# A hybrid SSM/attention layer on one core: squares summed before the token sums, loads and stores on other queues, weight copies in a later stage

## The chip, the cores and the metric

The kernel runs on one core of a Trainium2 chip as a single launch. The metric is the time of one execution on the device in microseconds (us), the median of three runs. The profile comes from one more execution of the same program, taken by the hardware profiler. The engines are PE (TensorE matmuls; PEld is its weight loading), DVE (VectorE), ACT (ScalarE), POOL (GpSimd) and SP (SyncE, which here only issues transfers); SPq, ACTq and POOLq are their issuing side.

## The reference

One layer for 1024 tokens of width 1024, everything in float32. Three sub-layers, each normalised ahead of it and behind it (RMSNorm) and added to the residual:

```python
# 1 token mixing: one input projection, whose columns are split
h = rms_norm(x, mix_pre_g)                  # -> u (512), q, k, v (512 each), f_logit (8)
y_s = s5_mixer(u)                           # diagonal SSM: 32 groups x 16 channels, 64 complex states
#     gelu, then  out = g * sigmoid(g @ glu_w + glu_b)
y_f = forgetting_attention(q, k, v, f)      # 8 heads x 64, causal, bias = cumsum(log_sigmoid(f))
x = x + rms_norm(concat(rms_norm(y_s), rms_norm(y_f)) @ w_out)
# 2 cross-attention into 256 memory tokens, 4 heads x 256
x = x + rms_norm(memory_cross_attention(rms_norm(x), mem_n, wq, wkv, wo))
# 3 FFN, hidden width 2816
x = x + rms_norm((silu(h @ w_gate) * (h @ w_up)) @ w_down)       # h = rms_norm(x)
```

`rms_norm(x, g)` is `x * rsqrt(mean(x*x) + 1e-6) * g`. What matters below is that the norms of `y_s` and `y_f` need, for each token, a sum of squares over 512 channels.

## The kernel before

Every float32 product is made of three matmuls on the parts of its operands: `split` (L112) makes a high part on ACT (L113) and the rest, the low part, on DVE (L115 or, with a gain, L117) or on POOL; `mm3` (L121) issues high·high, high·low and low·high. A weight is loaded into a `raw` tile, split into a `whl` tile, and used.

The program is written in the order of the layer, partly as generators that are advanced by `step`, `drain` and `paced`, and a scheduler then sets the order of each engine's instructions by its own timeline, dependences and priorities. Each engine works through its own list in order; a transfer sits in the list of the engine that issues it. An instruction without a dependence can be put very early. `tc.issue_after(x)` forbids an instruction to come ahead of `x`. Three names choose the engine that issues stores: `stA`, `stB`, `stC` (L149: POOL, SP, POOL).

Stages, with the times at which they stand in the trace: 0 to 57 us the projection `u` (x and `w_u` fetched row block by row block, `x_fetch`, `u_load` L259, `u_part`; `u_keep` L270 copies the eight accumulators into the SSM's input); 57 to 200 us q, k, v and the SSM; 200 to 229 us the SSM's output; 229 to 506 us the attention `fox` (L705) with *fillers* paced between its steps; 506 to 575 us the output projection (L1031 to L1051); to 612 us a product for cross-attention; 612 to 780 us cross-attention in eight turns (`xa_prep` L1067 reads the residual `x1` at L1069); 780 to 1220 us gate and up of the FFN; then down to the end.

`fox` goes through 8 heads times 8 query blocks: `scores` (PE into `s`, bias and row minimum on DVE L749, exponential on ACT L751, division on DVE or POOL, L756 or L754), two blocks later `turn` (PE transposes L769, split), then `values` (PE L780/L781) for two blocks at a time. `prepare(h)` fetches q, k (L720, L721) and the bias row `ncb` for a head and splits q and k on ACT, DVE and POOL. The fillers, in this order: half of v (`v1`), `glu` (L662), the SSM half of the output projection (`out_ssm`, whose result goes to DRAM as `t1_d`, L854), the normalised memory (`mem_load` L949, multiplied at L958), 16 key/value tiles of the memory (`mem_tile`, stored to `kv_d` at L972), and one of two products for the queries (`build_a`).

The sums of squares per token: `token_sums` (L233) takes a tile of squares, 128 channels by n·128 tokens, and multiplies each 128x128 block by a column of ones on PE (L237), then copies or adds the n columns into `sv` on DVE (L239, L241). `glu` calls it for each of four channel blocks and two token halves; `fox` calls it for every output of heads 0 and 1, while the squares of heads 2 to 7 are first added up in `sums[0]` (ACT, and POOL at L801) and multiplied by the ones once. `rsqrt_mean` (L127) turns a sum into 1/sqrt by ACT's Ln and Exp (L137, L138), which lie in another function table than `Tanh`, and one correction step on DVE.

In the FFN, `wd_sums` (L1335) makes for each of 22 half blocks of `w_down` three or fewer plain DRAM-to-DRAM copies into `wd_d` (L1339, 33 copies of 256 KB in all) and the differences of blocks on POOL. The copies have no dependence.

Of the kernel before, what the change touches and what calls it, by code (L numbers as in the profile page):

```python
# [52 lines left out]
def layer(ctx: ExitStack, tc: tile.TileContext, a, out):  # L53
# [95 lines left out]
    stA, stB, stC = pool, sp, pool  # L149
# [33 lines left out]
    t1_d = dram.tile([L, NC, D], F32, name="t1_d")  # L183
    kv_d = dram.tile([16, P, 256], F32, name="kv_d")
# [48 lines left out]
    def token_sums(sv, sq, first, p0=0, p1=P):  # L233
        n = sv.shape[1]
        ps = g_ps([P, n])
        for j in range(n):
            pe.matmul(ps[:, j:j + 1], sq[:, j * P:(j + 1) * P], ones[p0:p1, 0:1], start=True, stop=True)  # L237
        if first:
            dve.tensor_copy(sv, ps)  # L239
        else:  # L240
            dve.tensor_tensor(out=sv, in0=ps, in1=sv, op=ALU.add)  # L241
# [29 lines left out]
    def u_keep(us, banks):  # L271

        for j, ps in enumerate(banks):
            p = ps.rearrange("c (g i) -> c g i", i=16)
            act.activation(out=us[0][:, :, L - 1 - j], in_=p[:, 0:16], func=AF.Copy)
            dve.tensor_copy(us[1][:, :, L - 1 - j], p[:, 16:32])
        return us
# [385 lines left out]
    def glu(ys):  # L663
# [7 lines left out]
        sv = const.tile([P, NT], F32, name="sv_s")  # L671
        sq, sums = tt("d"), []
        for ct in range(4):
            cs = slice(ct * P, (ct + 1) * P)
            hl = slab([P, 2, S])
            for h in range(2):
                hs = slice(h * 512, h * 512 + 512)
# [13 lines left out]
                if h == 1:  # L691
                    ys.append(hl)
                yield
        token_sums(*sums.pop())
        ys_stat.append(sv)

    def glu_stats():
        sv, = ys_stat
        tables("natural_log_exp_and_others")
        rsqrt_mean(r_s, sv, 512, 4 * EPS)  # L700


    def fox(yf):
# [3 lines left out]
        def prepare(h):  # L707
# [4 lines left out]
            sp.dma_start(out=ncb, in_=nc_d[h:h + 1, :].broadcast_to([P, S]))  # L712
            heads[h] = (qs, ka, ncb)
            eng = dve if h < 2 else pool
            for hf in range(2):
                hs = slice(hf * 512, hf * 512 + 512)
                qk = tt("d" if h == 0 and hf else "e", [P, 2, 512])
                qd, kd = qk[:, 0], qk[:, 1]
                for rr in (0, 64):
# [878 lines left out]
```

## Time and profile before

| | before |
|---|---|
| median of 3 runs | 1435.04 us (1434.2, 1435.04, 2326.27) |
| the profiled execution, its own time | 1440.18 us |
| its span, first to last instruction | 1438.4 us, so 1.8 us lie around it |
| mean granted clock of TensorE | 0.989 |
| PE, DVE, ACT, POOL busy | 1395.6, 1002.3, 705.6, 398.4 us |
| transfers | 238.42 MB, mean 166 GB/s |

The profiled execution is 5.1 us (0.4%) longer than the median. In the tables of stretches below a row gives a stretch of the span, then the busy time (and count of instructions) of PE, PEld, DVE, ACT and POOL in it, then the granted clock as a share of the full one, the mean busy share of the DMA engines, and GB/s. In lists of waits the columns are the waiting engine and its line, who released it, total us, times, longest. In a timeline a row is start, duration, engine, line, operation, `out<-in`, and in brackets the idle time of that engine just before and who ended it.

### The profile page before, as it was taken

The numbers are of one execution on the slowest core, as the hardware profiler recorded it, in microseconds if no ns is written. First come the engines' busy times: TensorE is split into PE (matmuls) and PEld (weight loads), VectorE is DVE, ScalarE is ACT, GpSimd is POOL, SyncE is SP. The second block draws the span as 40 slices with busy tenths as digits, with TensorE's granted clock in tenths as the row PEclk, the third lists the DMA queues.
The fourth block names the chain that finished last, engine by engine and source line by source line (L and its number), as shares of the span: only waits on it lengthen the run. The fifth ranks groups of instructions, "written<-read, shape, count | busy, mean of one in ns | idle before, by whom it ended". The sixth has DMA issues, their size and how long they took to land.

```text
span 1438.4 us, 20783 instructions
## 1 busy us (share of the span) xinstructions
PE 1395.6 (97%) x7422; PEld 1191.4 (83%) x7422; DVE 1002.3 (70%) x1818; ACT 705.6 (49%) x1389; POOL 398.4 (28%) x432
## 2 busy tenths in 40 slices
PE   7999999999999899999999999999999899999997
PEld 6789898889989886788888788888888788888886
DVE  7848957887788877645457677777775766565565
ACT  6363347777888754543434533333333234444441
POOL 0000000022243135001021367667656621000021
PEclk9999999999999999999999999999999999999999
DMA  9625763165644658202327355554455425966544
GB/s 312 216 73 145 201 191 124 39 196 183 194 147 118 172 156 285 91 30 72 105 88 247 134 183 183 183 182 151 166 191 183 146 95 202 339 213 197 176 161 161
DMA packets 112823, 238.42 MB, mean 166 GB/s; under 512 B 11848, under 2 KB 48712, under 8 KB 112592
## 3 DMA queue, kind: packets, MB, share of 16 engines
q1 hardware_dynamic: 96576, 182.01, 39.2%
q0 software_dynamic: 16144, 55.09, 10.8%
q8 instruction: 58, 0.95, 0.3%
q14 instruction: 45, 0.37, 0.1%
HBM read 168.90 MB, written 76.81 MB: 171 GB/s over the span
## 4 chain that ended last, share of the span: by engine, by line
PE 59%; DMA 13%; DVE 11%; POOL 6%; issue 5%; ACT 5%; SPq 1%; DVEq 0%; POOLq 0%; ACTq 0%
PE x L1271 7%; PE x L1526 7%; PE g L1526 7%; PE g L1271 6%; PE g L122 6%; PE g L124 5%; PE g L123 5%; DMA wt<-in_w_down 5%; DMA wt_d<-wt 4%; POOL wt L1345 3%; PE x L123 2%; PE x L124 2%; PE x L122 2%; PE g L769 1%; ACT slab L113 1%
## 5 line engine op out<-in xcount | busy, mean ns | idle before, releaser
L1271 PE MATMUL x<-slab,op 128*128 128x512 f32 x984 | 235.2, 391 | 4.2 <-ACT ev L1287 3.6
L1271 PEld LDWEIGHTS x<-slab,op 128*128 128x128 f32 x984 | 185.7, 189 | 43.8 <-ACT ev L1287 4.1
L1271 PE MATMUL g<-slab,op 128*128 128x512 f32 x744 | 178.7, 389 | 0.0
L115 DVE TENSOR_TENSOR slab<-slab 128x1024 fp32r<-128x1024 f32 (+2 forms) x92 | 110.4, 1208 | 82.3 <-ACT slab L113 80.8
L1271 PEld LDWEIGHTS g<-slab,op 128*128 128x128 f32 x744 | 139.7, 188 | 29.0
L122 PE MATMUL g<-slab,whl 128*128 128x512 f32 (+1 forms) x416 | 151.6, 364 | 0.8 <-DVE slab L115 0.4
L123 PE MATMUL g<-slab,whl 128*128 128x512 f32 (+1 forms) x416 | 148.4, 357 | 0.0
L124 PE MATMUL g<-slab,whl 128*128 128x512 f32 (+1 forms) x416 | 148.0, 357 | 0.0
L113 ACT ACTIVATE slab<-slab 128x1024 fp32r<-128x1024 f32 (+2 forms) x92 | 95.0, 1037 | 104.4 <-DMA slab<-hs_d 81.2
L1526 PE MATMUL g<-slab 128*128 128x512 f32 x462 | 126.6, 389 | 0.0
L1526 PE MATMUL x<-slab 128*128 128x512 f32 x462 | 126.6, 389 | 0.0
L1526 PEld LDWEIGHTS g<-slab 128*128 128x128 f32 x462 | 86.7, 188 | 18.0
L1526 PEld LDWEIGHTS x<-slab 128*128 128x128 f32 x462 | 86.7, 188 | 18.0
L122 PE MATMUL g<-whl,slab 128*128 128x256 f32 (+2 forms) x288 | 86.0, 311 | 11.9 <-ACT whl L113 9.5
L1345 POOL TENSOR_TENSOR wt<-wt 128x256 f32<-128x256 f32 x88 | 73.3, 833 | 73.0 <-DMA wt<-in_w_down 70.6
L113 ACT ACTIVATE op<-ss 128x512 fp32r<-128x512 f32 x60 | 37.6, 629 | 106.3 <-PE g L1271 45.4
L115 DVE TENSOR_TENSOR whl<-raw,whl 128x1024 fp32r<-128x1024 f32 (+2 forms) x61 | 71.9, 1182 | 24.1 <-ACT whl L113 23.7
L122 PEld LDWEIGHTS g<-slab,whl 128*128 128x128 f32 x416 | 78.6, 189 | 12.1 <-ACT whl L113 0.6
L124 PEld LDWEIGHTS g<-slab,whl 128*128 128x128 f32 x416 | 78.4, 189 | 11.6 <-DVE whl L115 0.2
L123 PEld LDWEIGHTS g<-slab,whl 128*128 128x128 f32 x416 | 78.7, 189 | 10.5
L113 ACT ACTIVATE op<-slab 128x512 fp32r<-128x512 f32 x80 | 49.8, 626 | 76.6 <-PE x L1271 40.0
L123 PE MATMUL g<-whl,slab 128*128 128x256 f32 (+2 forms) x288 | 86.7, 301 | 0.0
(394 smaller groups left out, 3192.2 us busy)
## 6 DMA issues: line engine op xcount, KB each, us to landing
hs_d<-ev POOLq DMA_DIRECT2D x77, 256.0 KB, 3.0
slab<-hs_d SPq DMA_DIRECT2D x35, 512.0 KB
wt<-in_w_down SPq DMA_DIRECT2D x44, 256.0 KB
wt_d<-wt POOLq DMA_DIRECT2D x22, 512.0 KB, 3.5
slab<-in_w_gate SPq DMA_DIRECT2D x20, 512.0 KB
slab<-in_w_up SPq DMA_DIRECT2D x20, 512.0 KB
slab<-wt_d SPq DMA_DIRECT2D x20, 512.0 KB
wd_d<-in_w_down SPq DMA_DIRECT2D x33, 256.0 KB
```

What stands on the lines that cost most here:

```text
L113: first = act.activation(out=hi, in_=src, func=AF.Copy, scale=1.0 if mul is None else mul)
L115: (lo_eng or dve).tensor_tensor(out=lo, in0=src, in1=hi.bitcast(F32), op=ALU.subtract)
L122: pe.matmul(ps, lh, rh, start=first, stop=False)
L123: pe.matmul(ps, lh, rl, start=False, stop=False)
L124: pe.matmul(ps, ll, rh, start=False, stop=last)
L769: pe.transpose(tp[:, k], sc[:, (k0 + k) * P:(k0 + k + 1) * P], ident)
L1271: pe.matmul(ps, x[:, k], y[:, k], start=first and k + n == 0, stop=k == 3 and n == 2, skip_group_check=not first)
L1345: pool.tensor_tensor(out=o, in0=x, in1=y, op=ALU.subtract)
L1526: pe.matmul(banks[n][j], xo[:, u, js], wo[:, v], start=ends[0] and k == 0, stop=ends[1] and k == 2, skip_group_check=onto is not None)
```

## The change

Six edits:

1. `token_sums` is called on squares that were added up first. In `glu` the loops are turned round (token half outside, channel block inside); the squares of channel blocks 1 to 3 are added to those of block 0 on DVE, and `glu_sums(h)` multiplies by the ones once for each half. The scale of each half is computed as soon as its sums exist (`glu_stats`), that of the first half while the second is under way. The loads of the memory are held behind `glu`'s last addition by a one-column memset. In `fox` the squares of heads 0 and 1 go to DRAM (`sq_d`), come back as one tile at head 2, and heads 2 to 7 are added to it on POOL.
2. q, k and the bias row of heads 1 to 7 are fetched by POOL instead of SP, whole instead of in halves, k straight into the tile of its parts; from head 3 on they follow the latest POOL division (`mults`), which is that of the head before, block 1.
3. `stB` becomes ACT: the stores of `t1_d` and `kv_d`.
4. The 33 copies of `w_down` are held behind the reads of `x1` in cross-attention, 6 behind each of five and 3 behind a sixth.
5. The SSM is advanced by one step right after `u_keep`'s code and by two steps behind its fourth bank, instead of by three ahead of it. The copies of `u` so come ahead of these steps.
6. In the output projection the square of `x1` is written to an SBUF tile in four pieces of 256 columns, where it was written over the PSUM accumulator in two of 512; one reduction adds the four sums.

```diff
-    stA, stB, stC = pool, sp, pool
+    stA, stB, stC = pool, act, pool
...
         for j in range(n):
-            pe.matmul(ps[:, j:j + 1], sq[:, j * P:(j + 1) * P], ones[p0:p1, 0:1], start=True, stop=True)
-        if first:
-            dve.tensor_copy(sv, ps)
-        else:
-            dve.tensor_tensor(out=sv, in0=ps, in1=sv, op=ALU.add)
+            pe.matmul(ps[:, j:j + 1], sq[:, j * P:(j + 1) * P], ones[:, 0:1], start=True, stop=True)
+        dve.tensor_copy(sv, ps)
...
                 split(hl[:, 0, hs], hl[:, 1, hs], y, g_out[:, ct:ct + 1])
-                while sums:
-                    token_sums(*sums.pop())
-                act.activation(out=sq[:, hs], in_=y, func=AF.Square)
-                sums.append((sv[:, 4 * h:4 * h + 4], sq[:, hs], ct == 0))
+                act.activation(out=y if ct else sq[:, hs], in_=y, func=AF.Square)
+                if ct:
+                    glu_end[0] = dve.tensor_tensor(out=sq[:, hs], in0=sq[:, hs], in1=y, op=ALU.add)
+                if (h, ct) == (1, 1):
+                    glu_sums(0)
                 yield
...
+            with tc.issue_after(mults[-1].ins) if mults else ExitStack():
+                for rr in (0, 64):
+                    for t_, i in ((qd, 0), (kd, 4)):
+                        (pool if h else sp).dma_start(out=t_[rr:rr + 64], in_=qk_d[i + h // 2, r0:r0 + 64])
+                (pool if h else sp).dma_start(out=ncb, in_=nc_d[h:h + 1, :].broadcast_to([P, S]))
...
-            if h < HA:
-                act.activation(out=sq, in_=y, func=AF.Square)
-                later.append((sv[:, 2 * qc:2 * qc + 2], sq, h == 0, 64 - r0, P - r0))
+            act.activation(out=sq, in_=y, func=AF.Square)
+            if h < 2:
+                stC.dma_start(out=sq_d[64 - r0:P - r0, qs_], in_=sq)
                 return
-            if h == HA and qc == 0:
+            if h == 2 and qc == 0:
                 sums.append(tt("d"))
+                stC.dma_start(out=sums[0], in_=sq_d)
             total = sums[0][64 - r0:P - r0, qs_]
-            if h < HA + 2:
-                act.activation(out=total, in_=y, func=AF.Square)
-            else:
-                act.activation(out=sq, in_=y, func=AF.Square)
-                pool.tensor_tensor(out=total, in0=total, in1=sq, op=ALU.add)
+            pool.tensor_tensor(out=total, in0=total, in1=sq, op=ALU.add)
+            if h == NH - 1:
+                later.append((sv[:, 2 * qc:2 * qc + 2], sums[0][:, qs_]))
...
-        step(gs, 3)
-        u_c = u_keep(us, banks)
+        u_c, kept = u_keep(us, banks)
+        step(gs)
+        with tc.issue_after(kept.ins):
+            step(gs, 2)
...
+            with tc.issue_after(glu_end[0].ins):
+                dve.memset(m[:, 0, 0:1], 0.0)
             sp.dma_start(out=m, in_=a["memT"].rearrange("(k p) m -> p k m", p=P)[:, k:k + 4])
...
-            act.activation(out=ps, in_=t[:, hs], func=AF.Square, accum_out=ss2[:, h:h + 1])
+            for q in range(2 * h, 2 * h + 2):
+                act.activation(out=tt("yt", [P, 256]), in_=t[:, q * 256:q * 256 + 256], func=AF.Square,
+                               accum_out=ss4[:, q:q + 1])
...
-            sp.dma_start(out=wd_d[f, h, p], in_=a["w_down"][2 * p + f][:, h * 512:h * 512 + 512])
+            with tc.issue_after(x1_read[min(2 + k // 4, 7)].ins):
+                sp.dma_start(out=wd_d[f, h, p], in_=a["w_down"][2 * p + f][:, h * 512:h * 512 + 512])
```

How the instructions stand now. **SP at the start**, while `x` (`in_xT`) and `w_u` are being fetched; a row is a line, the operation and the tile, and x6 counts equal rows in a row. Before:

```order
L552 DMA h_d<-c 128x112
L1339 DMA wd_d<-in_w_down 128x512 x6
L205 DMA slab<-in_xT 128x1024
L262 DMA raw<-in_w_u 128x512
L205 DMA slab<-in_xT 128x1024
L1339 DMA wd_d<-in_w_down 128x512 x3
L262 DMA raw<-in_w_u 128x512
L1339 DMA wd_d<-in_w_down 128x512 x14
L262 DMA raw<-in_w_u 128x512
L1339 DMA wd_d<-in_w_down 128x512 x4
L262 DMA raw<-in_w_u 128x512
L1339 DMA wd_d<-in_w_down 128x512 x6
```

And now:

```order
L552 DMA h_d<-c 128x112
L206 DMA slab<-in_xT 128x1024
L260 DMA raw<-in_w_u 128x512
L206 DMA slab<-in_xT 128x1024
L260 DMA raw<-in_w_u 128x512 x3
L158 DMA raw<-in_w_f 128x1024
```

The last two blocks of `x` and the last four of `w_u` had 33 copies ahead of and between them, and now have none. The copies stand in cross-attention, six behind a read of `x1` (L1085, L1069 before).

**POOL in the attention**, around the first division of a later head (`c<-c,nlr`; `b` is the bias row, `e` holds q, `d` the squares). Before:

```order
L754 TENSOR_TENSOR c<-c,nlr 128x256
L801 TENSOR_TENSOR d<-d,yt 64x256
L754 TENSOR_TENSOR c<-c,nlr 128x512
L725 TENSOR_TENSOR a<-e,a 64x512
L115 TENSOR_TENSOR slab<-e,slab 128x512
L801 TENSOR_TENSOR d<-d,yt 64x256
```

And now:

```order
L758 TENSOR_TENSOR c<-c,nlr 128x256
L722 DMA e<-qk_d 64x1024
L722 DMA slab<-qk_d 64x1024
L722 DMA e<-qk_d 64x1024
L722 DMA slab<-qk_d 64x1024
L723 DMA b<-nc_d 128x1024
L802 TENSOR_TENSOR d<-d,yt 64x256
L758 TENSOR_TENSOR c<-c,nlr 128x512
L729 TENSOR_TENSOR a<-e,a 64x512
L115 TENSOR_TENSOR slab<-slab 128x512
L802 TENSOR_TENSOR d<-d,yt 64x256
```

Five transfers came in between the division of query block 1 and that of block 3.

**ACT in the filler `glu`**: `t<-g,glub` is the `Tanh`, `rsy` the Ln and Exp of the scale. Before, behind the last `Tanh`:

```order
L683 ACTIVATE t_2804<-g,glub 128x512
L113 ACTIVATE slab<-t_2805,gains 128x512
L689 ACTIVATE d<-t_2805 128x512
L113 ACTIVATE slab<-g 128x128
L152 ACT_TABLE_LOAD
L751 ACTIVATE c,nlr<-c,nlr 128x512
L724 ACTIVATE a<-e 128x512
L113 ACTIVATE slab<-e 128x512
L137 ACTIVATE rsy<-sv_s,epsc 128x8
```

And now, with two further `Tanh` instructions behind it:

```order
L685 ACTIVATE t_2638<-g,glub 128x512
L137 ACT_TABLE_LOAD
L137 ACTIVATE rsy<-sv_s,epsc 128x4
L113 ACTIVATE slab<-g 128x4x128
L138 ACT_TABLE_LOAD
L138 ACTIVATE rsy<-rsy 128x4
L113 ACTIVATE slab<-g 128x3x128
L113 ACTIVATE slab<-t_2639,gains 128x512
```

The scale of the first token half, which came behind all of `glu` and behind its table load, now stands between two `Tanh`, with two table loads more; the load at L152 remains.

More of the change, by code (lines that the diff above doesn't have):

```diff
@@ L809, in fox @@
         seq = [(h, t) for h in range(NH) for t in range(NT)]
-        HA, sums = 2, []
+        sums = []
         lag = 2
@@ L979, in fillers @@
         rows = out_ssm(ys)
-        glu_stats()
+        tables("natural_log_exp_and_others")
+        glu_stats(0)
+        for h in range(2):
+            for _ in range(2):
+                step(rows)
+                yield
+            if h == 0:
+                glu_sums(1)
+                glu_stats(1)
         for _ in mem_load(r_mem[0], mem):
```

74 lines of the change are left out of this document (36 added, 38 removed).

## The prediction

> **What bounds the kernel now.** First the page's list of busy time.
>
> ```profile
> PE 1395.6 (97%) x7422; PEld 1191.4 (83%) x7422; DVE 1002.3 (70%) x1818; ACT 705.6 (49%) x1389; POOL 398.4 (28%) x432
> ```
>
> PE is idle for 1438.4 - 1395.6 = 42.8 us in all. So an edit can win in three ways only: by less work on PE, by removing some of these 42.8 us, or by keeping the clock up. Second the table of 36 us stretches, of which these rows bear on the edits:
>
> ```profile
> 36.00:72.00 36.00, 33.90 (x151) 27.81 (x150) 31.72 (x101) 12.56 (x26) 0.96 (x1) 0.95 0.66 216
> 108.00:144.00 36.00, 36.00 (x277) 33.66 (x276) 31.41 (x69) 11.46 (x31) 3.53 (x7) 1.00 0.50 145
> 252.00:288.00 36.00, 33.45 (x217) 29.85 (x217) 30.55 (x74) 28.02 (x62) 3.42 (x2) 0.95 0.12 37
> 468.00:504.00 36.00, 32.22 (x222) 29.40 (x221) 30.18 (x65) 26.29 (x58) 6.60 (x7) 0.95 0.65 173
> 504.00:540.00 36.00, 33.89 (x189) 30.37 (x190) 28.13 (x47) 19.74 (x44) 12.53 (x10) 0.91 0.50 155
> 540.00:576.00 36.00, 32.64 (x134) 24.52 (x133) 28.25 (x47) 17.49 (x45) 17.76 (x15) 0.98 0.85 284
> 576.00:612.00 36.00, 35.26 (x157) 29.07 (x158) 24.40 (x48) 19.71 (x41) 0.45 (x1) 0.93 0.24 86
> 612.00:648.00 36.00, 36.00 (x173) 30.02 (x172) 15.76 (x49) 14.71 (x43) 0.53 (x1) 1.00 0.08 30
> ```
>
> The column behind POOL is the granted clock. Where PE sat idle for about 2 us, or several times in a row, it is below 1.00, so a stall costs its idle time and some slow matmuls after it. I price the slow part as (1 - clock) x 36: 1.8 us at 0.95, 3.2 us at 0.91, and 0.7 + 2.5 = 3.2 us for the pair 0.98 and 0.93. Third, what PE waited for:
>
> ```profile
> PE g L122 <- ACT whl L113: 9.9, 3, 7.4
> PE x L1271 <- ACT ev L1287: 3.6, 1, 3.6
> PE x L122 <- ACT x L1045: 2.4, 3, 0.9
> PE g L122 <- DVE slab L117: 2.3, 1, 2.3
> PE g L780 <- ACT slab L113: 2.3, 1, 2.3
> PE g L122 <- DVE sv_f L239: 1.8, 1, 1.8
> PE s L742 <- DVE nlr L749: 0.8, 1, 0.8
> ```
>
> 7.4 us of the first row is the head of the program, before PE's first matmul, and the second row lies in the FFN; no edit touches either. What is left is short and scattered.
>
> **Copies of w_down out of the start: -3.9 us.** The timeline of the start:
>
> ```profile
> 35.98 0.53 SPq L262 DMA_DIRECT2D raw<-in_w_u  x1
> 37.02 3.29 SPq L1339 DMA_DIRECT2D wd_d<-in_w_down  x4
> 43.64 0.63 ACT L113 ACTIVATE whl<-raw 128x512 fp32r<-128x512 f32 x1 [11.62 <-DMA raw<-in_w_u]
> 44.32 1.19 PE L122 MATMUL g<-whl,slab 128*128 128x512 f32 x4 [2.10 <-ACT whl L113]
> ```
>
> SP puts copies between the weight loads, a load issued at 35.98 lands only for 43.64, and PE stands 2.10 us. Without copies on SP or in the DMA engines there, these loads are ready early. I take the stall and its slow part: 2.1 + 1.8 = 3.9. The next stage is not starved (row 108: PE 36.00), so the gain is kept. The copies' new place costs nothing as I take it: four issues took 3.29 us, so six take about 4.9 us of a turn of (780 - 612) / 8 = 21 us, in a stage where the DMA engines are 0.08 busy at its start and PE 36.00. If nothing hid them, 33 x 0.82 = 27 us would come back.
>
> **Sums of squares: -9.0 us of PE time, -7 of it realised.** A group of four calls is eight instructions, and the next matmul starts 0.80 us later; a group on 64 rows takes 0.53 us:
>
> ```profile
> 251.03 0.95 PE L237 MATMUL g<-ones,d 128*128 128x1 f32 x8
> 251.83 0.31 PE L742 MATMUL s<-slab,a 128*128 128x128 f32 x1
> 257.70 0.60 PE L237 MATMUL g<-ones,yt 64*128 64x1 f32 x4
> 258.23 0.44 PE L769 MATMUL g<-ident,c 128*128 128x128 f32 x2
> 229.00:500.00 271.00, 259.32 (x1942) 239.91 (x1942) 224.22 (x501) 219.92 (x478) 67.53 (x59) 0.99 0.49 147
> ```
>
> `glu` goes from eight groups to two and heads 0 and 1 from eight small groups to none: 6 x 0.80 + 8 x 0.53 = 9.0 us. The eight calls at the end remain, in pairs. The last row is the attention as a whole: PE 259.3 of 271 us busy, DVE 224.2, ACT 219.9. PE is the limit on average, by 35 us, but all three engines hand each other work. So I take three quarters, and keep 0 and 9.0 as ends. DVE exchanges additions: six of 128x512 come in, at most half of the 1.86 us that L958 (below) takes for 128x1024, so 5.6 us, and eleven small ones go; I count that as hidden under PE.
>
> **The stall at 284: -3 us.** DVE's list held back both a sum's copy and the next block's row minimum behind the memory's multiplication:
>
> ```profile
> 277.17 1.28 ACT L152 ACT_TABLE_LOAD   x1
> 278.47 0.72 ACT L751 ACTIVATE c<-c,nlr 128x512 f32<-128x512 f32 x1
> 280.82 3.71 DVE L958 TENSOR_TENSOR raw<-raw,t 128x1024 f32<-128x1024 f32 x2 [0.81 <-ACT t L175]
> 284.52 0.15 DVE L239 COPY sv_f<-g 128x2 f32<-128x2 f32 x1
> 284.73 0.58 PE L122 MATMUL g<-whl,slab 128*128 128x256 f32 x1 [1.76 <-DVE sv_f L239]
> ```
>
> These sums exist no more, and the multiplication has other work of PE behind it. That is 0.8 + 1.76 of waiting and 1.8 of clock, -4.4. Against it stand two more table loads on ACT, 2 x 1.28 = 2.6 us, inside `glu`, with the splits and exponentials of the attention queued behind them; ACT is 28.02 of 36 busy there. I let half of them through: -4.4 + 1.3, about -3. Ends: -4.4 and, if the stall only moves and both loads show, +2.6. The Trainium skill, ScalarE: Activation LUTs, section "What ACT_TABLE_LOAD costs", puts a drain of about 1.38 us beside each load's 1.28 us. In this trace the instruction behind the load starts 1.30 us after it, with none of that drain to see. By the page the two loads would be 5.3 us and this term about -1.7 instead of -3.
>
> **x1's square off PSUM: -2 us.** It took 0.60 us and a read of 0.19 per half, and the accumulator was free only behind it: 2.4 us of waiting (third row above).
>
> ```profile
> L1045 ACT ACTIVATE x<-a x12: 592/601/602, 521.6 to 571.7; 128x512 f32<-128x512 f32 x12
> L1045 ACT ACTIVATION_READ_ACCUMULATOR x<-a x12: 185/188/198, 522.1 to 572.2; 128x1 f32 x12
> L791 ACT ACTIVATE yt<-yt x8: 414/417/418, 252.5 to 322.8; 64x256 f32<-64x256 f32 x8
> ```
>
> Now DVE's read frees it. ACT pays 4 x (0.42 + 0.19) - 2 x (0.60 + 0.19) = 0.9 us more a block, where it is 17.49 of 36 busy. Ends: -2.4 minus the pair's 3.2 of clock, and +1, since a wait for late weights stands in the same place.
>
> **Loads on POOL, stores on ACT: +1 us.** No wait of PE names the old loads. SP's waits are its own:
>
> ```profile
> SPq L720 <- POOL slab L115: 44.6, 8, 27.6
> SPq L972 <- ACT t L971: 29.9, 14, 5.7
> L972 SPq DMA_DIRECT2D kv_d<-t x16: 319/326/332, 306.8 to 378.8; - x16
> L854 SPq DMA_DIRECT2D t_d<-t x16: 360/366/589, 291.2 to 466.3; - x16
> L1322 POOL DMA_DIRECT2D hs_d<-ev x77 | 43.3, 575 | 77.8 <-DVE ev L1317 60.3 <-DVE ev L1332 16.4 <-issue 0.9
> 384.48 0.61 POOL L754 TENSOR_TENSOR c<-c,nlr 128x256 f32<-128x256 f32 x1 [12.03 <-DVE nlr L752]
> 392.73 1.04 POOL L754 TENSOR_TENSOR c<-c,nlr 128x512 f32<-128x512 f32 x1
> ```
>
> ACT gains 16 x 0.33 + 16 x 0.37 = 11.1 us of issuing over 271 us, and its slack there is 51. A store follows the ACT instruction that makes its data, so it waits for nothing else; what it delays are the splits queued behind, by 0.35 us each. Ends 0 and 11; I take +1. POOL gains 35 loads, eight stores and one load back, 44 x 0.575 = 25 us on 67.5 of 271, besides six additions. Five loads, 2.9 us, come between the divisions of blocks 1 and 3, which lie 392.73 - 384.48 - 0.61 = 7.6 us apart: hidden, 0. The loads come later than SP could send them, but the split that needs them stood long after. The other edit, copying `u` ahead of the SSM's steps, works in a stretch without a PE wait; I take 0, with 1 us either way.
>
> What I leave standing: the 2.3 us before L122 at 482 us (+1.8 of clock), the 2.3 us before L780 at 506 us (+3.2), both from transfers or DVE's list late in the attention, and the waits for late output weights near 574 us.
>
> **Sum:** -3.9 - 7 - 3 - 2 + 1 = -14.9 on the profiled 1440.2 gives 1425.3. That execution lies 5.1 us above the median of the runs shown, so against 1435.0 I predict 1420.
>
> **Rivals.**
> *The attention is tied by DVE and ACT, not PE.* They are 83% and 81% busy, in turns, and the new additions, table loads and issues fall on them. Then the 7 us and the stall's 3 turn into waits, and -3.9 - 2 + 1 is left: 1430. For it: rows 252 and 468, where PE has 33.45 and 32.22 while DVE has over 30. Against it: PE is at 96% of the whole.
>
> *The late stalls go too.* SP is free of 7 x 8 loads, 7 bias rows and 32 stores and can send the last weights sooner, so the stalls at 482, 506 and 574 vanish: 2.3 + 1.8, 2.3 + 3.2 and about 2.4 + 3.2, together 15.2 more: 1405. Against it: in 468 to 504 the DMA engines move 173 GB/s of the same bytes as before, and 0.85 of their time is taken in 540 to 576.
>
> *POOL's list becomes the bound: slower.* If one of the five loads takes longer than 7.6 / 5 = 1.5 us to issue, or waits for its buffer, the division of block 3 is late, and with it PE's transposes, in seven heads. A stall s that drops the clock costs 7 x (s + 1.8). At s = 3 that is 34: 1454. Waits well below 1.8 us kept the clock in this trace, so it decides near s = 1.8, where 7 x 1.8 = 12.6 jumps to 25 and passes the 14.9 gained; 2% slower is reached at s = 4.4, (14.9 + 28.7) / 7 - 1.8. The trace shows 0.575 us per issue beside a busy DVE (row of `hs_d`), which speaks against it. The Trainium skill, SBUF — State Buffer, section "SBUF: two separate sides", warns that a transfer issued from GpSimd is starved of descriptors while DVE runs certain copies, about 3100 ns instead of 620. By it five issues would take 15.5 us and s would be 7.9, so 1488; the 77 stores' mean of 575 ns shows nothing of the kind.
>
> *The copies do what they say, but elsewhere.* If they hold back the `x1` reads queued behind them, six turns lose up to 2 us each: 1432. The stage's idle DMA engines speak against it.
>
> **How the numbers follow.** Chances: forecast (1410 to 1428) 0.53; tied attention 0.20; late stalls go 0.13; POOL's list 0.08; copies 0.06. The range leaves out the lower half of the third and the slow cases beyond 1440: 1403 to 1438. About 2% is what a measurement here can tell from no change: below 1406 or above 1464. Below lies most of the third case, 0.12; above lies about half of POOL's, 0.05; the rest is 0.83.
>
> **What would show it.** Right: no PE wait near 44 us; 32 instructions at the ones' line instead of 112; the window from the first attention step to its last shorter by 8 to 10 us; no wait on a sum's copy near 284; no PE wait on the square in the output projection; PE full in cross-attention. Wrong: new PE waits on POOL's division or on ACT's split behind a store; waits on `nlr` inside `glu` behind a table load; POOL issues above 1.5 us; a late `x1` read; a stall at 482, 506 or 574 that grew or went.

## The result, and the profile after

| | before | changed |
|---|---|---|
| median of 13 runs each | 1435.63 us | 1444.31 us |
| ratio, 95% interval | | 1.0051 [1.0039, 1.0064] |
| the profiled execution, its own time | 1440.18 us | 1444.31 us |
| its span | 1438.4 us | 1442.5 us |

The change makes the kernel 0.5% slower: 7.3 us by the ratio, 8.7 by the medians; the forecast was 1420, with 1438 as the upper end. One of the 13 runs of before took 2326.27 us; the ratio leaves it out. The two profiled executions lie 4.1 us apart: the one of before was 4.6 above its 13 runs' median. What the traces account for is the 4.1; the rest is asked of the timed runs.

The page's list of busy time, of the changed kernel:

```profile
PE 1388.5 (96%) x7342; PEld 1181.8 (82%) x7342; DVE 999.0 (69%) x1823; ACT 709.0 (49%) x1427; POOL 426.3 (30%) x484
```

PE has 7.1 us less to do, as meant, and is idle for 1442.5 - 1388.5 = 54.0 us instead of 42.8. Its stretches, in the order of the rows shown of before:

```profile
36.00:72.00 36.00, 36.00 (x168) 30.10 (x167) 32.17 (x109) 12.35 (x27) 0.95 (x1) 1.00 0.31 93
252.00:288.00 36.00, 31.20 (x200) 27.50 (x200) 32.63 (x78) 31.04 (x66) 8.00 (x9) 0.95 0.31 93
540.00:576.00 36.00, 27.83 (x119) 22.21 (x119) 21.90 (x40) 13.85 (x48) 14.94 (x13) 0.94 0.79 242
612.00:648.00 36.00, 36.00 (x172) 29.99 (x171) 15.98 (x48) 14.33 (x40) 0.53 (x1) 1.00 0.22 72
```

The start is full now and cross-attention stays full with the copies in it (DMA share 0.22 instead of 0.08). The middle rows are emptier than before: 31.20 against 33.45 within the attention, 27.83 against 32.64 at the end of the output projection. What PE waits for, of the changed kernel:

```profile
PE g L122 <- ACT whl L113: 7.3, 2, 7.0
PE s L746 <- DVE nlr L753: 6.6, 6, 1.8
PE x L124 <- DVE b L115: 4.5, 1, 4.5
PE x L1287 <- ACT ev L1303: 4.4, 1, 4.4
PE x L122 <- DVE b L1058: 2.9, 1, 2.9
PE g L122 <- DVE yt L792: 2.3, 1, 2.3
```

Two rows are nearly as before (7.0 us at the head of the program, and the FFN's, 4.4 where it was 3.6). Four are new or have grown: the row minimum `nlr` of the attention (6.6 in six, where it was 0.8), `b` twice in the output projection, and `yt`, the tile in which a head's output is put together (2.3, where it was 1.2).

For the balance by stage three places on PE are compared, which have the same instructions in every kernel: the first product with the SSM's output, the first matmul of `build_a` (the last filler), and a group of twelve in the FFN. Timeline rows of before, then of the changed kernel:

```profile
203.10 0.38 PE L122 MATMUL g<-whl,slab 128*128 128x256 f32 x1 [0.46 <-ACT slab L649]
482.38 0.58 PE L122 MATMUL g<-a,whl 128*128 128x256 f32 x1 [2.30 <-DVE slab L117]
823.29 3.06 PE L1271 MATMUL x<-slab,op 128*128 128x512 f32 x12 [0.55 <-DVE op L115]
```

```profile
199.12 0.39 PE L122 MATMUL g<-whl,slab 128*128 128x256 f32 x1 [0.46 <-ACT slab L649]
478.99 0.39 PE L122 MATMUL g<-a,whl 128*128 128x256 f32 x1 [2.43 <-DVE slab L117]
827.54 3.02 PE L1287 MATMUL x<-slab,op 128*128 128x512 f32 x12 [0.55 <-DVE op L115]
```

Below, "attention" is the second less the first, "late" the third less the second, "rest" the span less the third. The last column holds the first and last read of the output projection's accumulators (`a<-x,r_f,a`), counted from the second place. The runs e1 to e18 are told below:

| kernel | start | attention | late | rest | first, last read |
|---|---|---|---|---|---|
| before | 203.1 | 279.3 | 340.9 | 615.1 | 38.1, 88.5 |
| changed | 199.1 | 279.9 | 348.6 | 615.0 | 32.2, 97.2 |
| e1, start (edits 4, 5) | 200.1 | 278.5 | 344.5 | 614.8 | |
| e2, x1 (6) | 203.7 | 277.6 | 342.4 | 614.4 | |
| e3, queues (2, 3) | 202.5 | 284.3 | 340.4 | 615.6 | |
| e4, `glu` part of 1 | 202.1 | 280.2 | 341.1 | 613.6 | |
| e6, loads (2) | 203.3 | 283.6 | 343.1 | 613.6 | |
| e7, stores (3) | 202.2 | 282.7 | 341.6 | 610.2 | |
| e8, `fox` part of 1 | 204.2 | 274.2 | 346.0 | 615.0 | 31.5, 93.6 |
| e9, 4, 5, 6 and `fox` part | 200.4 | 275.1 | 345.7 | 615.5 | 31.4, 94.4 |
| e10, ones-matmuls doubled | 203.1 | 286.1 | 345.3 | 617.4 | |
| e12, e9 and `glu` part | 198.8 | 283.7 | 349.7 | 616.5 | |
| e13, split end alone | 203.1 | 277.3 | 341.7 | 611.0 | 29.8, 89.4 |
| e14, e9 with the old end | 200.7 | 275.7 | 340.3 | 611.6 | 37.6, 88.1 |
| e15, one ones-matmul a group | 203.4 | 274.4 | 340.9 | 615.0 | |
| e16, changed with the old end | 201.6 | 280.4 | 341.7 | 614.4 | 38.0, 89.4 |
| e17, e6, head 1 on SP | 203.2 | 282.6 | 341.5 | 618.9 | |
| e18, e6 all on SP | 203.2 | 282.7 | 341.8 | 611.8 | |

So of the profiled 4.1 us the start gives back 4.0, the attention costs 0.6 where it should have been 8 to 10 shorter, and 7.6 are lost behind it, where 2 should have been gained.

### The profile page after: what moved, and what is told of

Same layout as the page of the kernel before. It is cut to its first block, busy times and chain, and to the rows that moved or that the text cites. A ratio compares the mean times of both kernels' runs of the same rounds, so it can differ in the third digit from the quotient of the medians.

```text
span 1442.5 us, 20631 instructions
## 1 busy us (share of the span) xinstructions
PE 1388.5 (96%) x7342; PEld 1181.8 (82%) x7342; DVE 999.0 (69%) x1823; ACT 709.0 (49%) x1427; POOL 426.3 (30%) x484
## 3 DMA queue, kind: packets, MB, share of 16 engines
q0 software_dynamic: 19792, 67.16, 14.1%
## 4 chain that ended last, share of the span: by engine, by line
PE 37%; DMA 10%; POOL 7%; issue 4%; DVE 1%; ACT 1%; SPq 0%; POOLq 0%; DVEq 0%; ACTq 0%
PE x L1543 7%; PE g L1543 7%; DMA wt<-in_w_down 5%; PE x L1287 5%; POOL wt L1362 4%; PE g L1287 4%; DMA wt_d<-wt 3%; PE x L123 2%; PE x L124 2%; PE x L122 2%; PE g L122 2%; PE g L124 2%; PE g L123 2%; POOL ss L1388 2%; POOL slab L1388 1%
## 5 line engine op out<-in xcount | busy, mean ns | idle before, releaser
L113 ACT ACTIVATE slab<-slab 128x1024 fp32r<-128x1024 f32 (+2 forms) x106 | 103.6, 982 | 103.9 <-DMA slab<-hs_d 81.8
L115 DVE TENSOR_TENSOR op<-ss,op 128x512 fp32r<-128x512 f32 x60 | 64.6, 1079 | 46.4 <-ACT op L113 45.9
L122 PE MATMUL g<-whl,slab 128*128 128x256 f32 (+2 forms) x288 | 87.6, 310 | 8.4 <-ACT whl L113 7.0
L113 ACT ACTIVATE op<-ss 128x512 fp32r<-128x512 f32 x60 | 37.6, 628 | 115.4 <-POOL ss L1388 67.4
L115 DVE TENSOR_TENSOR op<-slab,op 128x512 fp32r<-128x512 f32 x80 | 78.7, 991 | 17.2 <-ACT op L113 16.6
```

What stands on the lines that cost most here:

```text
L113: first = act.activation(out=hi, in_=src, func=AF.Copy, scale=1.0 if mul is None else mul)
L115: (lo_eng or dve).tensor_tensor(out=lo, in0=src, in1=hi.bitcast(F32), op=ALU.subtract)
L122: pe.matmul(ps, lh, rh, start=first, stop=False)
```

## The experiments

Executions of one kernel scatter by 4 to 17 us (e4's twelve: 1433.10 to 1449.84), so one profile is good for places and the interval for the size. Every kernel was timed beside runs of the kernel before, and the ratio is formed from both sets. It is not the quotient of the medians (e8: 1.0011, by the medians 1.0028); sizes in us below are the ratio's unless medians are named.

The column "rest" warns of the same. Behind the third place the lists of all five engines are the same, instruction for instruction, in all kernels of these runs, and yet that stretch takes 610.2 to 618.9 us. Most of the spread goes with one wait of PE for ACT's `ev` in the FFN, 1140 us or so into the program: 0.4 us in e7, 3.6 before, 6.4 in e17. A single span thus holds up to 9 us that no changed order in this stretch explains, and the stages are read one by one.

### Which edit costs: each by itself on the kernel before

e1 holds edits 4 and 5, e2 edit 6, e3 edits 2 and 3, e4 the `glu` part of edit 1.

> The kernel before with edits 4 and 5 alone (w_down copies held behind the x1 reads, u copied ahead of the SSM's steps). Theory L (late loss): the start's 4 us are a gain by themselves, and what was lost in the changed kernel was lost to other edits: 1431 to 1432 against 1435.6, no PE wait near 44 us. Rival C (copies): the copies' new place delays the x1 reads or the output projection before them, and the loss of about 8 us between 502 and 780 us is theirs: 1437 to 1444.

> The kernel before with edit 6 alone (square of x1 to SBUF in four pieces). Theory X: this edit is what made the output projection and the product after it longer (5.7 us more of waiting and slow clock there), by the order it gives to ACT and DVE: 1439 to 1444, with waits of PE on L1058 and on splits behind it. Rival: the edit does what was forecast, its 2.4 us of waits go, 1433, and the loss comes from elsewhere.

> The kernel before with edits 2 and 3 alone (q, k and bias loads issued by POOL, t1 and kv stores by ACT). Theory Q: SP's emptier list sends the output projection's loads in another order and beside other traffic, so the loss after 502 us is this edit's: 1439 to 1443. Rival: the queues carry no critical load, 1435 to 1437, and the output projection stays as before.

> The kernel before with the glu half of edit 1 alone (six groups of matmuls at the ones fewer, 4.8 us of PE work; six additions on DVE and two table loads on ACT more). Theory T (attention tied by DVE and ACT): the PE work saved comes back as waits on nlr and yt, time 1434 to 1438. Rival P (PE-bound): 1429 to 1431.

| | median | ratio to before [95%] |
|---|---|---|
| e1 | 1433.23 | 0.9983 [0.9966, 1.0000] |
| e2 | 1434.76 | 0.9995 [0.9977, 1.0013] |
| e3 | 1443.03 | 1.0051 [1.0026, 1.0075] |
| e4 | 1439.76 | 1.0036 [1.0011, 1.0061] |

The start's gain is there in e1's profile, 3.0 us; the time is 2.4 shorter, by the interval between 0 and 4.9. x1's square does neither good nor harm that can be told; the queues, put at +1, cost 7.3 us. In e3 the loss lies in the attention, not behind it: 5.0 us in the table. One place stands out, in e3's timeline:

```profile
243.87 1.05 PE L237 MATMUL g<-ones,d 128*128 128x1 f32 x8 [2.95 <-ACT d L689]
```

PE waits for a square of `glu`, which ACT makes.

### The halves: additions on POOL, loads, stores, `fox`

e5 is e4 with `glu`'s six additions on POOL; e6 edit 2 alone; e7 edit 3 alone; e8 the `fox` part of edit 1, with its new end.

```diff
-    glu_end[0] = dve.tensor_tensor(out=sq[:, hs], in0=sq[:, hs], in1=y, op=ALU.add)
+    glu_end[0] = pool.tensor_tensor(out=sq[:, hs], in0=sq[:, hs], in1=y, op=ALU.add)
```

> The glu half of edit 1 alone, as in the run of it before, but with its six additions of squares on POOL, which is idle between 237 and 280 us. Theory D: in the glu stretch DVE is the engine that is full (11.8 to 12.0 of each 12 us), so the additions on DVE cost there and the PE work saved is worth nothing; off DVE, 4 us come back: 1433 to 1436 against 1439.8 with them on DVE. Rival: the loss is in the two table loads and the turned loops, and the time stays at 1438 to 1441.

> Edit 2 alone: q, k and bias loads issued by POOL, stores left on SP. Theory N (POOL's list): the loads stand behind v's stores and divisions, the q split on ACT comes late for head 1 (ACT waited 1.2 us there and PE 2.95), and later heads' nlr waits come with it: 1439 to 1443, so that edit 2 carries all of the queues' loss. Rival S: the stores on ACT do it, and this run is at 1434 to 1436.

> Edit 3 alone: t1 and kv stores issued by ACT, 32 issues of about 0.35 us in the list of an engine that is 81% busy in the attention. Theory N: little, 1434 to 1437. Rival S: the stores delay splits and exponentials, nlr waits appear, 1439 to 1443.

> The attention half of edit 1 alone: the squares of heads 0 and 1 kept in DRAM and added on POOL, eight groups at the ones fewer, 4.2 us of PE work, and eight small DVE additions fewer. DVE is not loaded by it, so by theory D it is kept, at least in part: 1431 to 1434. Rival T (everything in the attention is tied): 1435 to 1437.

| | median | ratio to before [95%] |
|---|---|---|
| e5 | 1436.75 | 1.0011 [0.9991, 1.0030] |
| e6 | 1439.72 | 1.0039 [1.0017, 1.0061] |
| e7 | 1438.83 | 1.0028 [1.0012, 1.0043] |
| e8 | 1439.58 | 1.0011 [0.9995, 1.0028] |

Loads and stores cost each by itself. For the loads the timeline of before and then of e6 shows how (L724 is head 1's split of q, L689 the square in `glu`):

```profile
238.99 0.62 ACT L689 ACTIVATE d<-t 128x512 f32<-128x512 f32 x1
240.84 0.62 ACT L724 ACTIVATE a<-e 128x512 fp32r<-128x512 f32 x1
241.35 1.00 PE L237 MATMUL g<-ones,d 128*128 128x1 f32 x8
```

```profile
242.73 0.63 ACT L724 ACTIVATE a<-e 128x512 fp32r<-128x512 f32 x1 [1.10 <-DMA v_d<-a]
243.87 0.61 ACT L689 ACTIVATE d<-t 128x512 f32<-128x512 f32 x1
244.54 1.05 PE L237 MATMUL g<-ones,d 128*128 128x1 f32 x8 [2.83 <-ACT d L689]
```

The split now stands ahead of the square on ACT; its tile is still being stored (`v_d<-a`), and ACT waits 1.10 us. With it an exponential and a `Tanh` have come ahead of the square, which starts 4.9 us later than before, and PE, whose next matmul is the sum, stands for 2.83 us. No wait names a load. At the last sum of `glu` e6 is 4.4 us behind (281.88 instead of 277.50 us), and the whole attention is 4.3 longer, so this is the place where the loads cost.

e5 lies below e4, with overlapping intervals. That would fit additions that cost because DVE has no room for them. The 12 us rows of that stretch, the first of before, the others of the changed kernel:

```profile
241.00:253.00 12.00, 12.00 (x78) 10.40 (x77) 11.81 (x28) 10.06 (x20) 0.00 (x0) 1.00 0.30 84
```

```profile
237.00:249.00 12.00, 10.73 (x57) 8.52 (x56) 11.83 (x23) 10.38 (x20) 1.60 (x3) 1.00 0.21 50
249.00:261.00 12.00, 9.41 (x58) 7.88 (x57) 11.96 (x29) 9.82 (x19) 2.18 (x4) 1.00 0.34 94
273.00:285.00 12.00, 10.21 (x68) 9.32 (x66) 10.56 (x25) 9.90 (x23) 5.85 (x5) 0.86 0.41 126
```

In the changed kernel DVE is at 11.83 and 11.96 of 12 while PE has 10.73 and 9.41; before, one such row has DVE at 11.81 and PE still at 12.00, so a full DVE alone does not stop PE. And e5 speaks against the additions as the cause: with them on POOL, PE has 7.90 of 12 us from 253 to 265 at a clock of 0.74, where e4 has 8.71 at 0.72 and before 11.99 at 1.00. The `glu` part makes PE wait there, in e4 1.25 us for `yt`, 1.09 for a `Tanh` on ACT and 0.95 for a split on DVE; why is not shown.

In e8 the attention is 5.1 us shorter, about as the removed matmuls promise (its PE work was put at 4.2), and the stretch behind it 5.1 longer.

### Is it a limit: the good parts together, PE work doubled, transfers taken away

e9 joins edits 4, 5, 6 and the `fox` part. e10 is the kernel before with every ones-matmul issued twice (`for _ in range(2):`). e11 is e9 with `x` loaded for two of eight blocks only in the output projection (3.1 MB less; the others add the projection to itself). e12 is e9 with the `glu` part, its additions on POOL and without further table loads.

> Edits 4, 5 and 6 and the attention half of edit 1, without the edits that cost something alone (glu half, POOL loads, ACT stores). Theory F (the output projection waits for its transfers, so an earlier arrival there is waited off again): the attention ends 7 to 9 us earlier than before, near 475, and the FFN starts at 822 to 824 all the same, time 1433 to 1436. Rival P (what is gained ahead is kept): 1426 to 1429.

> The kernel before with every matmul at the ones issued twice into the same result: 112 instructions more, about 10.6 us of PE work in the attention, nothing else. Theory P (PE sets the pace there): 1444 to 1447. Theory T (DVE and ACT tie the attention, PE has slack) with F: less than half of it shows, 1436 to 1440.

> As the combined run, but the output projection doesn't load the residual x for six of eight blocks (3.1 MB left out) and adds the projection to itself instead; same arithmetic work. Theory F: with less traffic the t1 and weight loads land earlier, the waits near 505, 545, 555 and 573 shrink, 5 us or more come back: 1427 to 1430. Rival (the lists of DVE and ACT hold that stage, not the transfers): as the combined run.

> The combined run plus the glu half of edit 1 with its additions on POOL and its scale's Ln and Exp held behind the one table load, so no extra table loads. Theory F: the attention gets up to 4 us shorter and the end stays, 1433 to 1436. Rival P: 1423 to 1427, which would be faster than both kernels.

| | median | ratio to before [95%] |
|---|---|---|
| e9 | 1436.94 | 1.0004 [0.9985, 1.0022] |
| e10 | 1449.6 | 1.0091 [1.0066, 1.0117] |
| e11 | 1440.93 | 1.0029 [1.0007, 1.0051] |
| e12 | 1444.46 | 1.0064 [1.0039, 1.0088] |

e10 takes 13 us longer, by the interval 9.5 to 16.8. Its page, beside the 1395.6 of before:

```profile
PE 1408.6 (97%) x7534; PEld 1204.8 (83%) x7534; DVE 992.4 (68%) x1818; ACT 703.4 (48%) x1389; POOL 395.7 (27%) x432
```

13.0 us more work of PE came with 13 us more time (0.91% of 1435), but the stages do not say that the one is the other. 11.5 of the 13.0 lie in the attention, which is only 6.8 longer; the late stretch is 4.4 longer with 1.4 more work, the rest 2.3 with 0.4. Nor did PE's work alone change: the scheduler set DVE's and ACT's lists into another order too, from 242 us on. So e10 speaks against much slack in the attention and does not settle it.

e11 speaks against bandwidth as the cause of the late loss: with less traffic that stretch is 346.2 us, where e9 has 345.7. e9 comes to the second place 7 us earlier than before and gives 5 of them back behind it. e12 was expected to keep the gain without the additions' cost and does not: the attention is 8.6 us longer than e9's. So neither additions on DVE nor further table loads are needed for the `glu` part to cost; what is left of it is the turned loops and the order that they bring, and why that costs stays open.

### The late loss: the end of the attention

Edit 1 also changes the end of `fox`, which the prediction did not price: the last sums are done in pairs inside the last head, and `r_f` is computed for six blocks first, then for two. e13 puts only that end into the kernel before; e14 takes it out of e9.

```diff
-        token_sums(sv, sums[0], False)
-        rsqrt_mean(r_f, sv, 512)
+        rsqrt_mean(r_f[:, 0:6], sv[:, 0:6], 512)
+        token_sums(*later.pop(0))
+        rsqrt_mean(r_f[:, 6:8], sv[:, 6:8], 512)
```

e15 is the kernel before with one ones-matmul instead of a group, its column copied over (the other sums are left out): less PE work with the same instructions on DVE.

> The kernel before with one piece of edit 1 alone: at the attention's end the last sums are taken in four pairs and the scale r_f is made in two parts (columns 0 to 5, then 6 and 7), where before one group of eight and one scale stood. No PE work is saved, and the lists up to there stay as before; those of the output projection come out in the changed kernel's order. Theory E (this end is what makes the output projection longer by 5 to 8 us): 1439 to 1443, with PE's waits near 556 and 574 as in the changed kernel. Rival A (an earlier arrival is simply waited off at late transfers, whatever the order): 1434 to 1437, late stage as before.

> The combined run (edits 4, 5, 6 and the squares of heads 0 and 1 through DRAM and POOL), but with the end of the attention as it was before: one group of eight, one scale. Theory E: the 5 us gained in the attention and the 3 to 4 at the start are kept, the late stage is about 341 us again: 1428 to 1432, faster than both kernels. Rival A: 1434 to 1437 as in the combined run.

> The mirror of the doubled run: the kernel before, where each group at the ones does only its first block and the copy or addition spreads that column (the other sums are left out). 80 instructions and about 8 us of PE work fewer, the same number of DVE operations. Theory P (PE work saved in the attention is kept when DVE gets no more to do): 1426 to 1430. Theory T (it comes back as waits): 1433 to 1437.

| | median | ratio to before [95%] |
|---|---|---|
| e13 | 1439.65 | 1.0030 [1.0009, 1.0051] |
| e14 | 1431.17 | 0.9970 [0.9953, 0.9987] |
| e15 | 1433.81 | 0.9990 [0.9973, 1.0007] |

e15 is the counterpart to e10. Its page:

```profile
PE 1385.7 (97%) x7344; PEld 1180.2 (82%) x7344; DVE 997.4 (70%) x1818; ACT 703.4 (49%) x1389; POOL 394.6 (28%) x432
```

PE has 9.9 us less to do, and the time falls by 0.1%, 1.4 us, at most 3.9 by the interval. Here too the lists changed, and there are new waits of PE, the longest 2.83 us for a square at 279. Its attention is 274.4 us, where before has 279.3 and e13, with the same lists up to 490 us, 277.3.

The end alone makes the kernel before 0.30% slower, though its lists differ from those of before only between 490 and 595 us. Taking it out of e9 makes that 5.8 us faster by the medians, 4.9 by the ratios: e14 is faster than both kernels. The rows of `r_f`'s readers (count, duration in ns, first and last start, form), of before, of the changed kernel, of e9 and of e14:

```profile
L1044 DVE SCALAR_TENSOR_TENSOR a<-x,r_f,a x12: 736/743/752, 520.5 to 570.9; 128x512 f32<-128x512 f32 x12
```

```profile
L1058 DVE SCALAR_TENSOR_TENSOR a<-x,r_f,a x12: 737/747/752, 511.2 to 576.2; 128x512 f32<-128x512 f32 x12
```

```profile
L1047 DVE SCALAR_TENSOR_TENSOR a<-x,r_f,a x12: 739/748/751, 506.9 to 569.8; 128x512 f32<-128x512 f32 x12
```

```profile
L1044 DVE SCALAR_TENSOR_TENSOR a<-x,r_f,a x12: 737/746/751, 514.0 to 564.5; 128x512 f32<-128x512 f32 x12
```

With the old end the readers take 50 us from first to last (520.5 to 570.9, 514.0 to 564.5), with the split one 65 and 63. (In e15, also with the old end, it is 56, with the first read at 32.8 and a late stretch of 340.9: an early first read alone does not cost.) The first comes 6 to 8 us sooner after the second place; the last comes 5 to 9 us later in the changed kernel, e8 and e9. In e13's profile it is only 0.9 later; that execution was the fastest of its twelve and doesn't show the timed loss. PE's waits between 500 and 600 us, added up, are 6.3 (before), 7.8 (e14) and 7.3 (e16) with the old end; 10.3 (e13), 12.4 (e8), 10.0 (e9) and 14.1 (changed) with the split one. The two don't part cleanly: e1, with the old end, has 10.3 too, and a late stretch of 344.5. So the split end is not all that lengthens this stretch.

Which wait grows differs. In e13 it is PE's for the square over the accumulator, 2.4 us in three before:

```profile
PE x L122 <- ACT x L1046: 5.4, 3, 2.4
```

In the changed kernel (as in e9 and e12) DVE's list has changed at the last blocks. Its timeline, with PE's row behind it:

```profile
573.24 0.75 DVE L1058 SCALAR_TENSOR_TENSOR a<-x,r_f,a 128x512 f32<-128x512 f32 x1 [4.79 <-DMA a<-t_d]
573.90 0.68 DVE L115 TENSOR_TENSOR b<-t,b 128x512 fp32r<-128x512 f32 x1
574.64 0.51 PE L124 MATMUL x<-whl,b 128*128 128x512 f32 x1 [4.54 <-DVE b L115]
```

and DVE's of before:

```profile
565.31 1.01 DVE L115 TENSOR_TENSOR b<-t,b 128x512 fp32r<-128x512 f32 x1
568.39 0.74 DVE L1044 SCALAR_TENSOR_TENSOR a<-x,r_f,a 128x512 f32<-128x512 f32 x1
```

Before, the split of `b`, which PE needs, stands on DVE ahead of the reader that may have to wait for its `t1` load. Now it stands behind it: DVE waits 4.79 us for the load and PE 4.54 for the split. With the old end put back (e14, e16) the split is ahead again, DVE waits for `t1` too (2.73 and 3.53), and no PE wait on `b` is left. In the changed kernel, then, the loss goes with DVE's order, which the new end brings; a run that changes this order alone was not made.

### Does the same hold in the changed kernel, and what of the loads costs

e16 is the changed kernel with the old end. e17 is e6 with head 1's loads on SP (`pool if h > 1 else sp`); e18 has the loads in edit 2's form and all on SP.

> The changed kernel with the old end of the attention (one group of eight, one scale), everything else as changed. Theory E (the split end costs 4 to 5 us wherever it stands): 1439 to 1441 against 1444.3. Rival: the output projection's loss in the changed kernel comes from the queues as well, and the time stays at 1443 to 1446.

> Edit 2 alone, but with the loads of head 1 left on SP, so that only heads 2 to 7 are fetched by POOL. Theory H (head 1's loads stand among v's stores on POOL, the split of q waits on ACT for 1.2 us, PE for 2.8 at 244 us and its clock drops): most of the edit's 5.6 us go, 1435 to 1437. Rival: the later heads' loads cost, 1438 to 1441.

> Edit 2's new form of the loads (whole tiles, k straight into its parts' tile, held behind a division) with all of them left on SP. The orders of PE, DVE and ACT come out nearly as in the two runs with POOL loads, the q split of head 1 some rows earlier on ACT. Theory O (the order that the form gives costs, not the queue): 1438 to 1445, again with a wait of PE on L689 near 244 us. Rival Q (POOL as the issuing queue costs): 1434 to 1437.

| | median | ratio to before [95%] |
|---|---|---|
| e16 | 1440.78 | 1.0042 [1.0026, 1.0057] |
| e17 | 1445.2 | 1.0072 [1.0046, 1.0097] |
| e18 | 1444.62 | 1.0072 [1.0051, 1.0094] |

In e16's profile the late stretch is 341.7, as before, instead of 348.6; its median is 3.5 us under the changed kernel's, by the ratios only 1.3, with overlapping intervals, so that the old end helps there is not shown by the times. e18 refutes the queue: with every load back on SP the loss is no smaller (nor with head 1's alone, e17), and the same stall stands there, in e18:

```profile
244.45 1.05 PE L237 MATMUL g<-ones,d 128*128 128x1 f32 x8 [2.83 <-ACT d L689]
```

So it is the form of the loads (whole, behind a division, k into the tile of its parts). It acts by the order that it gives ACT, as far as the traces show: at the last sum of `glu` e18 is as far behind as e6, 281.86 us. Which part of the form does it was not taken apart, and why e17 and e18 cost more than e6 is open. In the profiles they do not cost more in the attention (282.6 and 282.7 against 283.6); the 7 us between e17's and e18's spans lie in the rest.

## Why the prediction was wrong, point by point

- **What bounds the kernel.** "By less work on PE" was taken to be a way to win by itself, and "PE is the limit on average" turned 9.0 us of PE work into 7 of time. This step failed first: with all edits PE has 5.9 us less to do in the attention, and the attention is 0.6 longer. By the times alone e15 keeps 1.4 us of 9.9, at most 3.9. e10 and e15 changed other lists too, so the price of one matmul stays open; PE's share of 97% does not give it.
- **Copies out of the start, -3.9.** Right in its stage: -4.0, PE full from 36 to 72, no wait near 44. Alone edits 4 and 5 give -0.17%, 2.4 us, between 0 and 4.9; how much of "so the gain is kept" held is not told by that. In e1's profile 3.6 us come back between the second and third place, all of it ahead of cross-attention: there PE is at 36.00 of 36 us in every row from 614 to 758 in e1, as in row 612 of the changed kernel. The copies' new place cost nothing, and the rival on copies fell.
- **Sums, -7.** The count on PE was right; the row of the ones in the changed kernel (instructions, us, mean ns):

```profile
L238 PE MATMUL g<-ones,d 128*128 128x1 f32 x32 | 4.1, 240 | 0.0
```

32 instead of 112, 4.1 us instead of 15.2. "I take three quarters" failed; whether the additions on DVE are "hidden under PE" is not told apart, since e12 loses without them. The `fox` half by itself did shorten the attention by 5.1 (e8), but the step left out its new end, which costs 0.30% (e13). The `glu` half costs 0.36% (e4), where 3.6 us of gain were counted in; the cause is open. With all edits the attention is not shorter at all (279.9 instead of 279.3): PE's busy time in it fell, its idle time rose by as much, as these windows of before and of the changed kernel say:

```profile
203.10:482.40 279.30, 268.75 (x2053) 250.23 (x2053) 216.92 (x487) 221.29 (x479) 67.44 (x60) 0.99 0.46 142
```

```profile
199.10:479.00 279.90, 262.82 (x1973) 243.03 (x1973) 223.34 (x485) 224.06 (x483) 95.49 (x111) 0.99 0.49 146
```

- **The stall at 284, -3.** The wait on a sum's copy went. In its place came a wait on DVE's row minimum, and the longest one on `yt` stands 36 us later:

```profile
279.17 0.50 PE L746 MATMUL s<-slab,a 128*128 128x512 f32 x1 [1.79 <-DVE nlr L753]
314.94 0.39 PE L122 MATMUL g<-slab,whl 128*128 128x256 f32 x1 [2.33 <-DVE yt L792]
```

  The clock at the first is 0.86 (row 273), as it was at the stall of before. That is what the first rival, the tied attention, says; its 1430 missed the queues and the end.
- **x1's square, -2.** Its PE waits are gone, others of the same accumulators (`b` by L1058, 2.9) came; alone -0.05%, not to be told from nothing.
- **Loads on POOL, stores on ACT, +1.** Mis-sized: 7.3 us together (e3). The argument counted issuing time and ACT's mean slack, and not which instruction waits ahead of which on ACT. The loads' new form moves a waiting split, an exponential and a `Tanh` ahead of a square that PE needs; the stores alone cost 0.28%, and "what it delays are the splits queued behind, by 0.35 us each" was too little. In e7's list of waits:

```profile
PE g L780 <- ACT t L851: 4.8, 3, 3.4
```

  Before it was 2.1 in two, the longest 1.2. PE waits there for the ACT instruction that reads its accumulator and makes a store's data. At the longest, which ends at 431 us, ACT had stood 3.67 us until 427 for a head's q (`e<-qk_d`; 1.64 before), with this read behind it: again a wait for a transfer ahead of something that PE needs, and more than an issue's length. Why that load landed later is not shown.
- **POOL's list.** Not the cause (eight additions came to it, not six). The loads' issues on POOL in the changed kernel (count, us, mean ns, idle before):

```profile
L722 POOL DMA_DIRECT2D e<-qk_d x14 | 7.6, 546 | 9.3 <-DVE a L729 8.2 <-PE g L657 1.2
```

  546 ns each beside a full DVE, far from the 1.5 us at which the rival would begin. The Trainium skill's about 3100 ns (SBUF — State Buffer, "SBUF: two separate sides") are for a transfer issued from GpSimd beside a DVE `tensor_copy`, and the prediction's 1488 took them for an issue; no issue here shows anything of the kind.
- **The table loads.** They take the 1.28 us, and ACT goes on 1.30 us after a load's start, as before. Whether they cost by themselves isn't told apart: e12, which has no further ones, is no faster. The rows of the first in the changed kernel:

```profile
259.80 1.28 ACT L137 ACT_TABLE_LOAD   x1
261.10 0.30 ACT L137 ACTIVATE rsy<-sv_s,epsc 128x4 f32<-128x4 f32 x1
```

- **The sum.** The edits' own ratios add up to -0.17 - 0.05 + 0.51 + 0.36 + 0.11 = +0.76%; all together are +0.51%. The sign was wrong because three terms were (sums, queues, and the end that had no term). No rival that went slower had this cause. Of the three late stalls in the rival "the late stalls go too", two stayed (2.43 us at 479, 2.46 at 502) and the one near 574 grew to 4.54.

**Open:** why the `glu` part costs, with its additions on DVE or off it; why e17 and e18 cost more than e6; how much of the changed kernel's late loss is the end alone (e16's times don't separate it); and the 4.6 us by which the profiled execution of before lies above its median (its "rest" is 4.9 us longer than e7's, with the same lists).

## What to carry to other kernels

Where engines work through fixed lists and three of them are about 80% busy or more in the same stage, an edit could not be priced by the busy time that it adds or removes; ask what its new order puts ahead of an instruction that another engine waits for. 7 us less on PE came with 7 to 9 us more in time here, and a part of an edit that did nothing but split one small step cost 0.3%. Every edit is then worth a run by itself, above all the part that looks too small to price: of six edits, four pieces (copies and `u` at the start, x1's square, the attention's squares with the old end) make 1431.2 us, 0.30% [0.13, 0.47] faster than before, and the rest cost more than they gave.

## What the runs showed of the hardware

- PE's busy time did not translate into time: 13.0 us added to many small places came with 13 us more (9.5 to 16.8), 9.9 us taken from the same places with 1.4 less (at most 3.9). The other engines' lists changed as well in both.
- The granted clock fell to 0.86 in the 12 us with one wait of 1.79 us (273 to 285), and stayed at 1.00 in the 12 us with waits of 1.12 and 1.47 us (249 to 261, rows above and here):

```profile
253.07 0.88 PE L773 MATMUL g<-ident,c 128*128 128x128 f32 x6 [1.12 <-ACT t L685]
255.42 0.44 PE L746 MATMUL s<-slab,a 128*128 128x384 f32 x1 [1.47 <-DVE nlr L753]
```

  In e4 waits of 1.25, 1.09 and 0.95 us between 254 and 259 went with 0.72 in 253 to 265, so the longest single wait does not tell the clock.

- Executions of one program on one chip scatter by 4 to 17 us (e16 1438.93 to 1443.32, e4 1433.10 to 1449.84), as much as the edits' effects and more. With the same lists in all engines, the stretch behind the third place took 610.2 us in e7's profile and 618.9 in e17's.
